# Recurrent mixer of a hybrid encoder: running values in PSUM banks, GELU as one table function, a fourth buffer of gate weights

## The chip, the cores and the metric

The kernel runs on one core of a Trainium2 chip. The metric is the device time of one execution in microseconds (us); the times below are the median, the lowest and the highest of three executions, and the time of one profiled execution. The engines are called as in the profile: PE (TensorE, matmul), DVE (VectorE), ACT (ScalarE), POOL (GpSimd), and SP, which issues the large transfers.

## What is computed

Input x has 256 tokens of 2048 channels, in fp32. There are two layers, each a token mixer followed by a SwiGLU feed-forward network, both with a residual. Mixer 0 is grouped-query attention; mixer 1, which the change touches, is a recurrent block:

```
xb, yb = split(h @ w_in)                       # 2 x 2048 channels
yb = gelu(yb, approximate=True)
xb = depthwise_conv_width_4(xb) + bias
for each direction d (forward, backward):
    r = sigmoid(xb @ w_a[d] + b_a[d])          # block diagonal, 8 blocks of 256 x 256
    i = sigmoid(xb @ w_i[d] + b_i[d])
    log_a = -8 * r * softplus(-lam[d]);  a = exp(log_a)
    u = sqrt(1 - a*a) * (i * xb)
    h_t = a_t * h_(t-1) + u_t                  # scan over the tokens
out = ((h_fwd + h_bwd) * yb) @ w_out
```

## The kernel before

Values lie with channels on the 128 partitions and the 256 tokens along the free axis, so one tile of 128 x 256 is a column of 128 channels. Matrix products run in two fp32r parts: a weight is split into hi and lo, an activation into a pair of halves, and three of the four products are summed. Weights stream in pieces of 512 KB (8 tiles of 128 x 128): a transfer on SP's queue (L92), a cast to hi on ACT (L93), a subtraction to lo on DVE (L94), with five buffers of each; PE follows. A product with 16 such tiles is 16 "steps".

In the recurrent mixer a column is projected by `project_sum`, 16 steps of three matmuls with 256 columns each (L166, L167, L168), into one half of a PSUM bank from the pool `acc` (4 banks). The mixer goes through 8 blocks of 256 channels, in 9 rounds: round b projects the two x columns of block b+1 (`conv_branch`) and then the two y columns of block b (`gelu_branch`), 64 steps in a full round, 240 matmuls with those of the gates.

- `conv_branch`: L535 brings the projection from PSUM to the tile cb, L537 (ACT) starts the convolution in xc, three operations of L539 (DVE) finish it, and `split` (L203, L204) makes xs, the input of the gates.
- `gelu_branch`: L547 brings y to SBUF, L549 (ACT) squares it, L550 (DVE) makes the argument of the sigmoid.
- `load_gates`: the weights of one gate (four per block: two of the decay, two of the input) by SP (L563), cast ghi on ACT (L564), glo on POOL (L565); three buffers of ghi and glo, two of the raw weights graw. The load of gate n+3 is written behind the matmuls of gate n.
- `Block.gates`: 12 matmuls into a PSUM bank of the pool `pm` (4 banks), then Sigmoid (sg); for the gates 2 and 3 a product with xc on POOL (L599), for the gates 0 and 1 a Tanh into th.
- `decay`: Exp and Square (L610) on ACT, L611 on DVE. `scan`: Sqrt on ACT, then L616 and the scan L619 or L621 on DVE, and h+h of both directions on POOL (L622).
- `gelu`: the table of Sigmoid is loaded (L576), Sigmoid of each y's argument, a product on POOL (L580) into gl. `finish`: a product on POOL (L627), and `split` makes the input of the output projection. In the last block the products of `gelu` and `finish` and h+h are on DVE (`self.eng`).

All functions that go through a table are issued by `table_act`, whose line is L298, and keep their written order; the load of a table stands on L298 too, except L576. PE's order is written by hand: `later(t, fn)` puts a piece of a block's work t steps after the start of its round (WHEN; WHEN_LAST in the last). Gates come at the steps 18, 25, 32 and 39, scans at 58 to 64, the end of the block at 66 to 74, so in the following round. The other engines take the order that a scheduler lays down at build time, and each works its queue in that order. The output projection (`output`) needs the last two columns only after 44 steps.

Of the kernel before, what the change touches and what calls it, by code (L numbers as in the profile page):

```python
# [14 lines left out]
AF = mybir.ActivationFunctionType  # L15
ALU = mybir.AluOpType
# [3 lines left out]
S = 256  # L20
D = 2048
KT = D // P
# [8 lines left out]
EPS = 1e-6  # L31
LRU_C = 8.0
GRID_W = 64
GELU_C = 0.7978845608028654

FRONT = 4
FIRST = 1
# [2 lines left out]
VALUE = 32  # L40
USUAL = (17, 22, 15, 7)
LATE = ((10, 23, 15, 13), (4, 15, 17, 9))
GATE_BUFS = 3
WHEN = (18, 25, 32, 39, 42, 46, 50, 54, 58, 60, 62, 64, 66, 70, 74)
WHEN_LAST = (5, 9, 13, 17, 19, 20, 21, 24, 24, 25, 26, 27, 33, 39, 39)
GELU_B = 0.044715

PK = {}
_o = 0
# [10 lines left out]
def trunk(ctx, tc, w, out):  # L60
    nc = tc.nc
    act, dve, pool, pe, sync = nc.scalar, nc.vector, nc.gpsimd, nc.tensor, nc.sync
# [87 lines left out]
    def new_acc():  # L150
        return ps_a.tile([P, 2 * S], F32, tag="acc", name=nm("acc"))
# [16 lines left out]
        pe.matmul(o, lo, x[:, :S], start=False, stop=stop)  # L168

    def project_sum(xs):  # L170
        acc = new_acc()[:, :S]
        for k0 in range(0, len(xs), HALF):
            for k, (hi, lo) in enumerate(half(), k0):
                three(acc, hi, lo, xs[k], k == 0, k == len(xs) - 1)
                step()
        return acc

    def output(xs, ready, norm, close):
        accs = [new_acc() for _ in range(FRONT)]
# [22 lines left out]
    def split(dst, src):  # L202
        dve.tensor_copy(dst[:, :S], src)  # L203
        dve.tensor_tensor(dst[:, S:], src, dst[:, :S].bitcast(F32), ALU.subtract)  # L204
# [3 lines left out]
    x_sb = [xq[k // 4][:, k % 4, :] for k in range(KT)]  # L208
# [13 lines left out]
    def col(name, i):  # L222
        o = PK[name] + i
        return pk[:, o : o + 1]
# [63 lines left out]
    def table_op(i):  # L288
        if prev[0] is not None:
            tc.add_manual_dep(  # L290
                i.ins, prev[0].ins.name,
                mybir.DependencyInfo(mybir.DependencyClass.NoSync, mybir.DependencyReason.DATA),
                reason="activation tables",
            )
        prev[0] = i

    def table_act(*a, **k):
        table_op(act.activation(*a, **k))  # L298
# [193 lines left out]
    def ffn(l, norm, nxt):  # L492
        def unit(i):
            g = evac(project(norm.xs), "fg")
            dve.tensor_tensor(g, g, norm.r, ALU.mult)
            table_act(g, g, AF.Silu)
            pool.tensor_tensor(g, g, norm.r, ALU.mult)  # L497
            u = evac(project(norm.xs), "fu")
            dve.tensor_tensor(u, u, g, ALU.mult)
            h = act_tile()  # L500
            split(h, u)
            return h

        bounds = np.cumsum([0] + PARTS)
        hid = [unit(i) for i in range(PARTS[0])]
        for p, n in enumerate(PARTS):
            last = p == len(PARTS) - 1
            cur = hid
            hid = [] if last else [unit(bounds[p + 1])]
            for j in range(KT):  # L510
                if last and j == KT - 1:
                    dve.tensor_tensor(x_sb[j], x_sb[j], project_sum(cur), ALU.add)
# [15 lines left out]
    rt = ctx.enter_context(ExitStack())  # L528
    scope.append(rt.enter_context(tc.tile_pool(name="rp", bufs=2)))
    def conv_branch(ct):  # L530
        acc = project_sum(nr.xs)
        b = tmp("cb", (P, S + 4))
        pool.memset(b[:, 0:2], 0.0)
        pool.memset(b[:, S + 2 : S + 4], 0.0)
        dve.tensor_tensor(b[:, 2 : S + 2], acc, nr.r, ALU.mult)  # L535
        xc = tmp("xc", bufs=4)
        act.activation(xc, b[:, 0:S], AF.Identity, bias=col("conv_b", ct), scale=col("conv_w", ct))  # L537
        for k in range(1, 4):
            dve.scalar_tensor_tensor(xc, b[:, k : k + S], col("conv_w", KT * k + ct), xc, ALU.mult, ALU.add)  # L539
        xs = tmp("xs", (P, 2 * S), F32R, bufs=4)  # L540
        split(xs, xc)
        return xc, xs

    def gelu_branch(ct):
        acc = project_sum(nr.xs)
        y = tmp("fg")
        dve.tensor_tensor(y, acc, nr.r, ALU.mult)  # L547
        t = tmp("fu")
        act.activation(t, y, AF.Square)  # L549
        dve.scalar_tensor_tensor(t, t, 1.0 / GELU_B, y, ALU.add, ALU.mult)  # L550
        return y, t


    gate_w = {}
# [13 lines left out]
    class Block:  # L568
        def __init__(self, b):
            self.b = b  # L570
            self.eng = pool if b < NBLK - 1 else dve
            self.xcs, self.ys, self.gls = [], [], []
            self.gate, self.th, self.hs = {}, {}, {}

        def gelu(self):
            table_op(act.preload_act_table_set("sigmoid_and_others"))  # L576
            for y, t in self.ys:
                table_act(t, t, AF.Sigmoid, scale=2.0 * GELU_C * GELU_B)
                gl = tmp("gl")
                self.eng.tensor_tensor(gl, y, t, ALU.mult)  # L580
                self.gls.append(gl)

        def gates(self, g):
            b = self.b
            hi, lo = gate_w.pop(4 * b + g)
            pst = ps_m.tile([P, 2 * S], F32, tag="pm", name=nm("pm"))
            for j in range(2):
                o = pst[:, j * S : (j + 1) * S]
                for k in range(2):
                    m = 2 * k + j  # L590
                    x = self.xcs[k][1]
                    three(o, hi[:, m, :], lo[:, m, :], x, k == 0, k == 1)
# [30 lines left out]
            self.hs.setdefault(j, h)  # L623

        def finish(self, j):
            h = self.hs[j]
            self.eng.tensor_tensor(h, h, self.gls[j], ALU.mult)  # L627
# [97 lines left out]
```

## Time and profile before

| | |
|---|---|
| median of 3 executions (lowest to highest) | 2129.33 us (2128.39 to 2139.98) |
| the profiled execution, its own time | 2129.33 us |
| its span in the trace (1.7 us lie outside) | 2127.6 us |
| busy: PE, DVE, ACT, POOL | 2085.5, 1502.9, 1050.4, 473.4 us |
| granted PE clock, mean over the span | 0.993 |
| PE in the stretch from 1063.3 to 1142.4 us | 79.10 of 79.10 us busy |
| PE in the stretch from 1142.4 to 1271.2 us | 120.34 of 128.80 us busy |
| PE in the stretch from 1271.2 to 1315.2 us | 36.63 of 44.00 us busy |

The page says that PE is busy for 98% of the whole span, which is a mean over stages. The recurrent mixer lies between 1063 and 1315 us: the last three rows are three stretches of it, and there PE is not always busy. A busy PE at a lower granted clock is busy for longer with the same work. Matmuls overlap in the trace, so the work of a stretch is best counted by the starts of its matmuls.

### The profile page before, as it was taken

The page shows a single profiled execution, that of the slowest core. Times are in us where ns is not written, and L with a number is a line of the kernel's source. Part 1 is how long each engine was busy: PE and PEld are TensorE (multiplying, and loading weights), DVE is VectorE, ACT ScalarE, POOL GpSimd, SP SyncE. Part 2 cuts the span into 40 slices and gives each one's busy share as a digit, 9 for nine tenths or more (in the row PEclk, how much of TensorE's full clock was granted, in tenths as well). Part 3 has the DMA queues.
Part 4 walks back from the last instruction along what each step waited for, and adds up shares of the span by engine and source line. Part 5 has one row for each costly group of instructions (what it writes and reads, how often), then busy time and mean ns, then how long its engine had stood idle before and what let it go on. Part 6 is the DMA issues. An engine that isn't in the chain of part 4 may idle for free.

```text
span 2127.6 us, 32676 instructions
## 1 busy us (share of the span) xinstructions
PE 2085.5 (98%) x12512; PEld 1848.4 (87%) x12512; DVE 1502.9 (71%) x2192; ACT 1050.4 (49%) x1598; POOL 473.4 (22%) x454
## 2 busy tenths in 40 slices
PE   7899999999999999999999998999999999999999
PEld 6788888888888888888999997888888888888888
DVE  8899876666566666668889898866666566666665
ACT  5465544443344434444587877454443444444442
POOL 5564431110011100113345553411110011001100
PEclk9999999999999999999999999999999999999999
DMA  6433655555555555555645454555555555665564
GB/s 239 146 122 118 203 187 189 185 185 186 187 188 188 173 186 195 188 183 177 196 160 169 161 166 157 185 188 190 190 194 189 189 189 187 183 203 190 188 189 138
DMA packets 112045, 384.27 MB, mean 181 GB/s; under 512 B 12560, under 2 KB 14736, under 8 KB 111888
## 3 DMA queue, kind: packets, MB, share of 16 engines
q1 hardware_dynamic: 111744, 382.17, 54.4%
q8 instruction: 98, 1.61, 0.3%
q14 instruction: 59, 0.48, 0.1%
q10 hardware_dynamic: 144, 0.02, 0.0%
HBM read 380.04 MB, written 2.10 MB: 180 GB/s over the span
## 4 chain that ended last, share of the span: by engine, by line
PE 86%; DVE 6%; issue 3%; ACT 2%; DMA 1%; POOL 1%; SPq 0%; ACTq 0%; DVEq 0%; POOLq 0%
PE acc L155 53%; PE acc L156 27%; DVE lo L94 2%; DMA graw<-in_w_gates_dram 1%; PE acc L168 1%; PE acc L167 1%; ACT sg L298 1%; PE acc L166 1%; PE pm L167 1%; POOL hb L351 1%; DVE xc L539 1%; PE pm L168 1%; DVE h L621 1%; ACT hi L93 1%; PE pm L166 1%
## 5 line engine op out<-in xcount | busy, mean ns | idle before, releaser
L94 DVE TENSOR_TENSOR lo<-raw,hi 128x1024 fp32r<-128x1024 f32 (+2 forms) x721 | 901.0, 1250 | 509.0 <-ACT hi L93 495.8
L93 ACT CAST hi<-raw 128x1024 fp32r<-128x1024 f32 (+2 forms) x721 | 740.8, 1029 | 928.2 <-PE acc L155 533.6
L155 PE MATMUL acc<-xg,hi 128*128 128x512 f32 x3200 | 1133.1, 398 | 5.7 <-ACT hi L93 5.7
L156 PE MATMUL acc<-xg,lo 128*128 128x256 f32 x3200 | 900.7, 281 | 5.4 <-DVE lo L94 5.4
L155 PEld LDWEIGHTS acc<-xg,hi 128*128 128x128 f32 x3200 | 603.4, 189 | 144.3 <-ACT hi L93 5.7
L155 PE MATMUL acc<-act,hi 128*128 128x512 f32 x1892 | 664.9, 396 | 4.6 <-DVE act L204 4.6
L156 PEld LDWEIGHTS acc<-xg,lo 128*128 128x128 f32 x3200 | 607.8, 190 | 7.1 <-DVE lo L94 7.0
L156 PE MATMUL acc<-act,lo 128*128 128x256 f32 x1892 | 530.9, 281 | 0.4 <-DVE lo L94 0.4
L155 PEld LDWEIGHTS acc<-act,hi 128*128 128x128 f32 x1892 | 355.8, 188 | 87.8 <-DVE act L204 5.5
L497 POOL TENSOR_TENSOR fg<-fg,nr 128x256 f32<-128x256 f32 x88 | 126.1, 1433 | 1189.9 <-ACT fg L298 1189.9
L156 PEld LDWEIGHTS acc<-act,lo 128*128 128x128 f32 x1892 | 358.4, 189 | 0.7 <-DVE lo L94 0.7
L168 PE MATMUL acc<-xg,lo 128*128 128x256 f32 x512 | 146.0, 285 | 3.0 <-DVE lo L94 3.0
L166 PE MATMUL acc<-xg,hi 128*128 128x256 f32 x512 | 146.4, 286 | 2.2 <-ACT hi L93 2.2
L167 PE MATMUL acc<-xg,hi 128*128 128x256 f32 x512 | 145.9, 285 | 0.0
L168 PEld LDWEIGHTS acc<-xg,lo 128*128 128x128 f32 x512 | 99.2, 194 | 3.8 <-DVE lo L94 3.8
L166 PEld LDWEIGHTS acc<-xg,hi 128*128 128x128 f32 x512 | 99.2, 194 | 3.1 <-ACT hi L93 3.1
L167 PEld LDWEIGHTS acc<-xg,hi 128*128 128x128 f32 x512 | 99.1, 194 | 0.0
L280 DVE TENSOR_TENSOR x<-x,acc 128x256 f32<-128x256 f32 x126 | 52.9, 420 | 57.8 <-PE acc L156 57.8
L254 POOL TENSOR_TENSOR ss<-ss,sq 128x256 f32<-128x256 f32 x60 | 78.1, 1302 | 4.9 <-ACT sq L250 0.7
L252 POOL TENSOR_TENSOR sq<-x 128x256 f32<-128x256 f32 x45 | 34.6, 769 | 114.6 <-DVE x L281 112.6
L244 DVE SCALAR_TENSOR_TENSOR xg<-x,pk,xg 128x256 fp32r<-128x256 f32 x64 | 56.2, 891 | 5.2 <-POOL xg L243 5.2
L351 POOL TENSOR_TENSOR hb<-hy,rope 32x256 f32<-32x256 f32 x60 | 46.1, 769 | 44.7 <-DVE hv L419 37.9
(164 smaller groups left out, 1486.6 us busy)
## 6 DMA issues: line engine op xcount, KB each, us to landing
raw<-in_w_gate_dram SPq DMA_DIRECT2D x176, 512.0 KB, 3.6
raw<-in_w_up_dram SPq DMA_DIRECT2D x176, 512.0 KB, 3.6
raw<-in_w_down_dram SPq DMA_DIRECT2D x128, 512.0 KB, 3.6
raw<-in_w_in_dram SPq DMA_DIRECT2D x64, 512.0 KB, 4.0
raw<-in_w_down_dram SPq DMA_DIRECT2D x64, 384.0 KB, 3.1
raw<-in_w_qv_dram SPq DMA_DIRECT2D x40, 512.0 KB, 3.7
raw<-in_w_o_dram SPq DMA_DIRECT2D x32, 512.0 KB, 3.6
raw<-in_w_out_dram SPq DMA_DIRECT2D x32, 512.0 KB, 3.7
```

The source lines that it names most:

```text
L93: act.copy(hi[:, sl, :], raw[:, sl, :])
L94: dve.tensor_tensor(lo[:, sl, :], raw[:, sl, :], hi[:, sl, :].bitcast(F32), ALU.subtract)
L155: pe.matmul(acc, hi, xs[k], start=(k == 0), stop=False)
L156: pe.matmul(acc[:, S:], lo, xs[k][:, :S], start=False, stop=(k == total - 1))
L166: pe.matmul(o, hi, x[:, :S], start=start, stop=False)
L167: pe.matmul(o, hi, x[:, S:], start=False, stop=False)
L168: pe.matmul(o, lo, x[:, :S], start=False, stop=stop)
L244: dve.scalar_tensor_tensor(t[:, S:], x_sb[k], g, t[:, :S].bitcast(F32), ALU.mult, ALU.subtract)
L254: pool.tensor_tensor(self.ss, self.ss, sq, ALU.add)
L280: dve.tensor_tensor(x_sb[j], x_sb[j], acc[:, :S], ALU.add)
L351: eng.tensor_tensor(b[32 * j : 32 * j + 32], y[32 * i : 32 * i + 32], s[32 * i : 32 * i + 32], ALU.mult)
L497: pool.tensor_tensor(g, g, norm.r, ALU.mult)
```

## The change

`project_sum` gives back, beside the half of the bank that holds the product, the other half, `run`. The running sum of the convolution lives there, and only its last step writes xc to SBUF; y lives there too (for the last two columns in SBUF, as the output projection takes all four banks then). L549 and L550 go. The GELU is one function from a table of its own, in place, in `run`. The Tanh's result th stays in the gate's PSUM bank, in place of the sigmoid's input, and with it L611's, the square root's and L616's results. The product of `finish` goes to DVE and its result into `run`, from where it is split; the products L580 and L627 on POOL go. The sigmoid's table is no longer loaded by L576: the loads stand where a function of another set follows, which makes four in a block (Sigmoid with Tanh, Exp, Sqrt, Gelu) where there were three. The gate weights have four buffers of ghi and glo.

```
-GATE_BUFS = 3
+GATE_BUFS = 4
...
     def project_sum(xs):
-        acc = new_acc()[:, :S]
+        bank = new_acc()
+        acc = bank[:, :S]
...
-        return acc
+        return acc, bank[:, S:]
...
-        acc = project_sum(nr.xs)
+        acc, run = project_sum(nr.xs)
...
-        act.activation(xc, b[:, 0:S], AF.Identity, bias=col("conv_b", ct), scale=col("conv_w", ct))
+        act.activation(run, b[:, 0:S], AF.Identity, bias=col("conv_b", ct), scale=col("conv_w", ct))
         for k in range(1, 4):
-            dve.scalar_tensor_tensor(xc, b[:, k : k + S], col("conv_w", KT * k + ct), xc, ALU.mult, ALU.add)
+            o = xc if k == 3 else run
+            dve.scalar_tensor_tensor(o, b[:, k : k + S], col("conv_w", KT * k + ct), run, ALU.mult, ALU.add)
...
     def gelu_branch(ct):
-        acc = project_sum(nr.xs)
-        y = tmp("fg")
+        acc, y = project_sum(nr.xs)
+        if ct >= KT - 2:
+            y = tmp("gl")
         dve.tensor_tensor(y, acc, nr.r, ALU.mult)
-        t = tmp("fu")
-        act.activation(t, y, AF.Square)
-        dve.scalar_tensor_tensor(t, t, 1.0 / GELU_B, y, ALU.add, ALU.mult)
-        return y, t
+        return y
...
         def gelu(self):
-            table_op(act.preload_act_table_set("sigmoid_and_others"))
-            for y, t in self.ys:
-                table_act(t, t, AF.Sigmoid, scale=2.0 * GELU_C * GELU_B)
-                gl = tmp("gl")
-                self.eng.tensor_tensor(gl, y, t, ALU.mult)
-                self.gls.append(gl)
+            for y in self.ys:
+                table_act(y, y, AF.Gelu_apprx_tanh)
...
-                    self.th[g, j] = tmp("th", bufs=4)
+                    self.th[g, j] = pst[:, j * S : (j + 1) * S]
...
         def finish(self, j):
-            h = self.hs[j]
-            self.eng.tensor_tensor(h, h, self.gls[j], ALU.mult)
-            split(g_t[2 * self.b + j], h)
+            y = self.ys[j]
+            dve.tensor_tensor(y, self.hs[j], y, ALU.mult)
+            split(g_t[2 * self.b + j], y)
```

PE's order stays, and so do the places of the casts and loads of weights in the queues of ACT and SP. Inside a block the scheduler lays the operations of ACT and DVE otherwise. ACT's queue from a block's square roots to the next convolution reads so before; hi and ghi are casts of weights, th the roots, fu the GELU's arguments:

```order
L93 CAST hi_11397<-raw_11396 128x1024
L298 ACT_TABLE_LOAD
L298 ACTIVATE th_10943<-th_10943 128x256
L298 ACTIVATE th_10997<-th_10997 128x256
L298 ACTIVATE th_10947<-th_10947 128x256
L298 ACTIVATE th_11001<-th_11001 128x256
L576 ACT_TABLE_LOAD
L298 ACTIVATE fu_11157<-fu_11157 128x256
L93 CAST hi_11492<-raw_11491 128x1024
L549 ACTIVATE fu_11249<-fg_11247 128x256
L93 CAST hi_11547<-raw_11546 128x1024
```

In the changed kernel the lines have lower numbers; pm_10911 and pm_10963 are the banks of the forward and the backward direction, each with the columns 0 and 1, and acc_11046 and acc_11141 hold the two y:

```order
L297 ACT_TABLE_LOAD
L297 ACTIVATE pm_10911<-pm_10911 128x256
L297 ACTIVATE pm_10963<-pm_10963 128x256
L91 CAST hi_11460<-raw_11459 128x1024
L297 ACTIVATE pm_10911<-pm_10911 128x256
L91 CAST hi_11515<-raw_11514 128x1024
L297 ACTIVATE pm_10963<-pm_10963 128x256
L297 ACT_TABLE_LOAD
L297 ACTIVATE acc_11046<-acc_11046 128x256
L297 ACTIVATE acc_11141<-acc_11141 128x256
L91 CAST hi_11555<-raw_11554 128x1024
L536 ACTIVATE acc_11229<-cb_11298,pk 128x256
```

The four roots, which stood together, now have a weight cast before the third and before the fourth; the third waits until DVE has scanned column 0 of its own bank, the fourth likewise. Both GELUs stand together behind their table.

DVE's queue at the same place before, from the first scan on (lo is a weight's subtraction, cb the next block's convolution):

```order
L619 SCALAR_TENSOR_TENSOR h_11213<-sg_1975_10941,th_10943 128x256
L621 SCALAR_TENSOR_TENSOR h_11223<-sg_1986_10995,th_10997 128x256
L619 SCALAR_TENSOR_TENSOR h_11234<-sg_1977_10945,th_10947 128x256
L621 SCALAR_TENSOR_TENSOR h_11244<-sg_1988_10999,th_11001 128x256
L94 TENSOR_TENSOR lo_11493<-raw_11491,hi_11492 128x1024
L550 SCALAR_TENSOR_TENSOR fu_11249<-fu_11249,fg_11247 128x256
L94 TENSOR_TENSOR lo_11548<-raw_11546,hi_11547 128x1024
L535 TENSOR_TENSOR cb_11326<-acc_11252,nr_10276 128x256
L203 CAST act_10217<-h_11213 128x256
```

And in the changed kernel, where L622 is the product of `finish`, with the result in the y's bank:

```order
L614 SCALAR_TENSOR_TENSOR h_11194<-sg_1968_10930,pm_10911 128x256
L92 TENSOR_TENSOR lo_11461<-raw_11459,hi_11460 128x1024
L616 SCALAR_TENSOR_TENSOR h_11204<-sg_1977_10982,pm_10963 128x256
L611 TENSOR_TENSOR pm_10911<-pm_10911,sg_1984_11031 128x256
L92 TENSOR_TENSOR lo_11516<-raw_11514,hi_11515 128x1024
L614 SCALAR_TENSOR_TENSOR h_11215<-sg_1969_10933,pm_10911 128x256
L611 TENSOR_TENSOR pm_10963<-pm_10963,sg_1997_11096 128x256
L622 TENSOR_TENSOR acc_11046<-h_11194,acc_11046 128x256
L534 TENSOR_TENSOR cb_11298<-acc_11229,nr_10276 128x256
L616 SCALAR_TENSOR_TENSOR h_11225<-sg_1978_10985,pm_10963 128x256
L202 CAST act_10217<-acc_11046 128x256
```

The scans, which stood in a row, are apart, with weights' subtractions between them; the product of column 0 stands ahead of the next convolution's start cb and of the last scan.

More of the change, by code (lines that the diff above doesn't have):

```diff
@@ L33 @@
 GRID_W = 64
-GELU_C = 0.7978845608028654
 FRONT = 4
@@ L42 @@
 LATE = ((10, 23, 15, 13), (4, 15, 17, 9))
-GATE_BUFS = 3
+GATE_BUFS = 4
 WHEN = (18, 25, 32, 39, 42, 46, 50, 54, 58, 60, 62, 64, 66, 70, 74)
 WHEN_LAST = (5, 9, 13, 17, 19, 20, 21, 24, 24, 25, 26, 27, 33, 39, 39)
-GELU_B = 0.044715
 PK = {}
@@ L511, in ffn @@
                 if last and j == KT - 1:
-                    dve.tensor_tensor(x_sb[j], x_sb[j], project_sum(cur), ALU.add)
+                    dve.tensor_tensor(x_sb[j], x_sb[j], project_sum(cur)[0], ALU.add)
                     if nxt is not None:
@@ L571, in __init__ @@
             self.eng = pool if b < NBLK - 1 else dve
-            self.xcs, self.ys, self.gls = [], [], []
+            self.xcs, self.ys = [], []
             self.gate, self.th, self.hs = {}, {}, {}
         def gelu(self):
-            table_op(act.preload_act_table_set("sigmoid_and_others"))
-            for y, t in self.ys:
-                table_act(t, t, AF.Sigmoid, scale=2.0 * GELU_C * GELU_B)
-                gl = tmp("gl")
-                self.eng.tensor_tensor(gl, y, t, ALU.mult)
-                self.gls.append(gl)
+            for y in self.ys:
+                table_act(y, y, AF.Gelu_apprx_tanh)
         def gates(self, g):
```

## The prediction

> **What bounds the kernel now.** I read the page first. PE is busy for 98% of the span, so a change off PE can only win where PE waits. The windows view of the recurrent mixer shows where that is (columns: us, then busy time and instructions of PE, of its weight loads, of DVE, ACT and POOL, the granted PE clock, DMA share, GB/s):
>
> ```profile
> PE 2085.5 (98%) x12512; PEld 1848.4 (87%) x12512; DVE 1502.9 (71%) x2192; ACT 1050.4 (49%) x1598; POOL 473.4 (22%) x454
> 1063.30:1142.40 79.10, 79.10 (x665) 79.10 (x664) 68.44 (x96) 62.99 (x113) 40.71 (x46) 1.00 0.52 170
> 1142.40:1271.20 128.80, 120.34 (x973) 118.09 (x973) 116.05 (x162) 102.76 (x182) 68.74 (x70) 0.99 0.50 164
> 1271.20:1315.20 44.00, 36.63 (x231) 33.37 (x231) 35.65 (x57) 34.17 (x62) 12.82 (x13) 0.90 0.40 133
> ```
>
> In the first stretch PE runs without a gap: 79.10/665 = 0.119 us a matmul, so a block of 240 matmuls takes 28.5 us. In the second it needs 128.80 us for 973, which at 0.119 are 115.7: 13.1 lost. In the tail 36.63 us are busy at a clock of 0.90, worth 33.0 at full clock: 11.0 lost of 44.0. **The most that this change can win is therefore about 24.1 us, 1.1% of the time.**
>
> The chain of waits over the stage returns at the same place in each block, the exponentials of the decay; the first and the last of seven:
>
> ```profile
> 1079.73 0.95 ACT sg L298 x3
> ...
> 1271.22 0.95 ACT sg L298 x3
> ```
>
> Six periods of 31.92 us: longer than PE's 28.5. So PE, which had run ahead of the others, is held from 1142 on by a loop on the other engines. PE's waits between 1043 and 1325 us name its outlets (total, times, longest):
>
> ```profile
> PE pm L168 <- POOL glo L565: 4.2, 4, 1.1
> PE acc L155 <- DVE act L204: 3.7, 1, 3.7
> PE acc L168 <- DVE lo L94: 3.0, 4, 0.8
> PE pm L166 <- ACT ghi L564: 2.3, 1, 2.3
> ```
>
> Gate weights come late, then weights, and at the end the last column of the mixer. One period of the chain shows what sets all of them (start, us, what):
>
> ```profile
> 1146.03 0.97 DVE lo L94
> ...
> 1149.73 0.34 DVE fu L550
> 1150.07 1.13 DVE lo L94
> ...
> 1155.22 1.17 DVE h L621
> ...
> 1157.50 0.88 DVE fu L550
> ...
> 1164.45 0.40 DVE xc L539
> ...
> 1164.85 0.34 DVE act L204
> ...
> 1165.99 2.09 issue
> ...
> 1168.56 4.89 DMA graw<-in_w_gates_dram
> ...
> 1173.55 0.62 ACT ghi L564
> ...
> 1174.93 1.28 ACT L298
> ...
> 1178.90 1.24 DVE lo L94
> ```
>
> DVE has no gap from 1146.03 until it frees a raw buffer at 1168.5 (22.5 us); SP, whose queue is in order, then gets to the gate's load (5.05 until ACT takes it); ACT casts it, and what stands behind in its queue follows (two sigmoids, a table load, the exponentials, a weight cast: 5.35), and DVE starts its next stretch at 1178.90. The sum is 32.87.
>
> **Part by part: DVE's stretch.** Some of DVE's time there is inflated. The "2.09 issue" is the end of a subtraction that took twice its time while POOL subtracted too; the timeline has the pair at 1134, and the groups show a quiet stage (480 to 640 us) against the recurrent one:
>
> ```profile
> 1134.11 1.31 POOL L565 TENSOR_TENSOR glo<-graw,ghi 128x512 fp32r<-128x512 f32 x1
> 1134.20 2.31 DVE L94 TENSOR_TENSOR lo<-raw,hi 128x1024 fp32r<-128x1024 f32 x1
> ```
> ```profile
> L94 DVE TENSOR_TENSOR lo<-raw,hi x57: 1224/1225/1226, 481.3 to 639.6; 128x1024 fp32r<-128x1024 f32 x57
> ```
> ```profile
> L94 DVE TENSOR_TENSOR lo<-raw,hi 128x1024 fp32r<-128x1024 f32 x40 | 55.6, 1391 | 15.8 <-ACT hi L93 15.8
> L616 DVE TENSOR_TENSOR th<-th,sg 128x256 f32<-128x256 f32 x20 | 7.5, 418 | 0.3
> L627 POOL TENSOR_TENSOR h<-h,gl 128x256 f32<-128x256 f32 x10 | 13.6, 1364 | 0.4
> L580 POOL TENSOR_TENSOR gl<-fg,fu 128x256 f32<-128x256 f32 x10 | 12.9, 1287 | 47.4 <-ACT fu L298 47.4
> ```
> ```profile
> L535 DVE TENSOR_TENSOR cb<-acc,nr x10: 409/411/416, 1128.3 to 1264.3; 128x256 f32<-128x256 f32 x10
> ```
> ```profile
> L539 DVE SCALAR_TENSOR_TENSOR xc<-cb,pk,xc x30: 472/839/1518, 1131.1 to 1267.8; 128x256 f32<-128x256 f32 x30
> ```
>
> An operation with two inputs in SBUF swings by a factor of three (L539), one with an input in PSUM stays within 409 to 416 ns whatever POOL does (L535). The change gives every DVE operation of this stretch but the subtractions of weights and the xs split an input in PSUM, and takes 2 of POOL's 13.6 us and 2 of its 12.9 us groups away: (13.6 + 12.9)/5 = 5.3 us a block.
>
> So I add the stretch up again at the undisturbed steps, from start to start: 7 weight subtractions at 1.13 (the row at 1150.07) are 7.9; 3 operations of L539 at 0.40 (at 1164.45) are 1.2; 18 small ones (4 of L611, 4 of L616, two evacuations, two products of `finish`, two splits and the xs split of two operations each) at 0.34 (at 1164.85) are 6.1; the four scans at 0.60, by a row of the tail:
>
> ```profile
> 1303.39 0.60 DVE h L619
> ```
>
> are 2.4. That makes 17.6, with the two products that come over from POOL (0.7) in it, and without L550, which took 0.34 + 0.88. What the subtractions still lose to POOL is today 7 x (1.391 - 1.225) = 1.2; a third of POOL's work goes, so I keep 0.8 (bounds 0 and 1.2). DVE's stretch becomes 18.4 instead of 22.5.
>
> *The price of PSUM.* About 22 of these operations read or write a PSUM bank that they did not. The nearest rows are L535, from PSUM, with 411 ns, against L616, from SBUF alone, with 418: I take zero. The widest gap between like operations of the two kinds is ACT's, 463 ns for a sigmoid from PSUM and 510 for a Tanh from SBUF:
>
> ```profile
> L298 ACT ACTIVATE sg<-pm,pk 128x256 f32<-128x256 f32 x40 | 17.5, 463 | 0.0
> L298 ACT ACTIVATE th<-sg,cs 128x256 f32<-128x256 f32 x20 | 10.2, 510 | 0.5
> L298 ACT ACT_TABLE_LOAD x10 | 12.8, 1283 | 0.2
> ```
>
> Taken in both directions, 22 x 0.047 = 1.0 us a block either way. [...]
>
> **ACT.** L549 goes (two a block) and a fourth table load of 1.28 us (the 1283 ns above) comes; the GELU takes the sigmoid's place. ACT was busy for some 25.4 us of a period (102.76/128.80 x 31.92) and stays under 26.8, so it fits a block. The new load, the sigmoid's, stands behind the cast of a gate's weights, right behind the convolution's start. ACT's timeline there, from the convolution that DVE's cb releases to the weight cast that DVE needs next:
>
> ```profile
> 1160.49 0.60 ACT L537 ACTIVATE xc<-cb,pk 128x256 f32<-128x256 f32 x1 [1.66 <-DVE cb L535]
> ...
> 1162.78 1.03 ACT L93 CAST hi<-raw 128x1024 fp32r<-128x1024 f32 x1
> ```
>
> is 3.3 us, with the load 4.6. DVE's own work between, one subtraction (1.13), three of L539 (1.2) and five small ones (1.7), comes to 4.0, so DVE waits 0.6 there (bounds 0 and 1.28). The third and fourth root each wait for a scan and the product of `finish` for the GELU; between them DVE has a weight subtraction (1.13) and ACT a cast, which cover the handshakes, and I price them at nothing; the rival below prices them uncovered.
>
> **The gate weights.** The fourth buffer means that each load, at its old place in the queues of SP and ACT, serves one gate later. That takes PE's waits on glo and ghi (4.2 + 2.3). But ACT's cast still stands in the same row and still waits for the same transfer, so the transfer and what follows it stay in the loop: 5.05 + 5.35. The extra first load lies before the feed-forward network, where DVE waits for ACT anyway; 0 to 1 us, I take 0.
>
> **New waits of PE.** The matmuls of gate 2 need the bank whose last reader is now the scan of forward, column 1:
>
> ```profile
> 1158.61 0.28 PE L166 MATMUL pm<-xs,ghi 128*128 128x256 f32 x1
> ```
>
> In the period shown all but the last scan have ended by 1155.3, so 3.3 us are left. A y column needs the bank that `finish` of the block before splits. From its first matmul to that split the loop runs over 7 steps and two gates, ACT's sigmoids and exponentials, and DVE's stretch up to the split (about 14 us): some 24 to 25 us, under the 28.5 of a block. Both are covered as long as DVE gains; uncovered, each would cost its lag once, not per block.
>
> **The sum.** 18.4 + 5.05 + 5.35 + 0.6 = 29.4 us a loop against 31.92 (this period had 32.87, so 29.4 is rather high): 6 x 2.5 = 15.1 us by the last exponentials. In the last block DVE sheds two of L550 and two of L580 from its chain:
>
> ```profile
> 1302.98 0.41 DVE fu L550
> ...
> 1305.17 0.40 DVE gl L580
> ```
>
> with 0.88 for the first L550, as at 1157.50, and 0.34 for the second product that is 2.0. Together 17.1 us of the 24.1 that PE loses: **2129.3 - 17.1 = 2112.2 us**. The profiled execution is the median of the runs, so nothing is to be converted. With the bounds (0 or 1.2 of contention, 1.0 of PSUM either way, 0 to 1.28 for the load) the loop lies between 27.0, where PE's 28.5 holds, and 31.5: 2105 to 2125.
>
> **The rivals.** *PE becomes the bound.* If the weight subtractions lose nothing more, or PSUM is a little cheaper, the loop falls under 28.5, PE runs as in the first stretch, and the tail shrinks as well: 2129.3 - 24.1 = 2105.2. For it speaks that the shown period was a long one; against it, that ACT gets up to 26.8 us busy of 28.5 and still has waits for DVE and for the transfer.
>
> *The loop stays.* The gate's transfer and the queue of ACT hold the block, and what POOL no longer reads, its subtractions and h+h take from DVE at other places (every weight subtraction can still go to 2318 ns). The loop is then 31, DVE's relief being lost but for one us: 6 x 0.9 + 2.0 = 7.4 less, some 2122, or with no relief at all 2127. For it speaks that ACT's idle time before the gate's cast is a wait for the transfer, which is not touched.
>
> *Slower: ACT's queue.* ACT works in order. Its third and fourth root now wait for scans with a weight subtraction ahead of each on DVE, and every weight cast behind them waits too, so that DVE lacks its next subtraction. If both handshakes lie bare, with subtractions at their longest (2.31 at 1134.20), the loop is 29.4 + 4.6 = 34.0: 6 x 2.1 - 2.0 = 10.6 slower, 2140. It decides from 2.5 us of bare wait a block. Against it speaks that ACT has idle time and five hi buffers. [...]
>
> **How the numbers follow.** The forecast has 0.42, PE as the bound 0.28, the loop that stays 0.21, slower 0.09. A measurement of this kernel can tell about 0.5%, 10.6 us, from no change. The first two cases lie under 2118.7, but for the upper end of the first, which the lower part of the third makes up: faster 0.69. Between 2118.7 and 2140.0 lie the third and half of the last: same 0.26; slower 0.05. The range goes from 2104, PE's bound with 1 us for its estimate, to 2126, the upper end of the forecast and all of the third case but its no relief at all.
>
> **What would show it.** Right: L539, the scans and the split at 0.40 to 0.70 us with no swing; periods of the exponentials at 29 to 29.8; PE's waits on glo and ghi gone; four loads of 1283 ns a block. Wrong: periods over 31 with DVE idle before weight subtractions and ACT idle before roots or casts (the third case or the last); PSUM operations of over 0.5 us; PE waiting for the bank of a y column or of gate 2 in every block.

## The result and the profile after

The changed kernel takes 2105.43 us (median of 4 executions, 2104.81 to 2106.43), the kernel before 2128.86 (2128.05 to 2139.98). The ratio is 0.9892, with a 95% interval of 0.9846 to 0.9937: 1.1% faster. The forecast was 2112.2 with a range of 2104 to 2126; the time came out where the rival "PE becomes the bound" had put it, 2105.2.

The windows view of three stretches of the recurrent mixer, after, from the first gate on (columns as before):

```profile
1063.00:1142.40 79.40, 79.40 (x667) 79.40 (x666) 62.14 (x103) 71.50 (x123) 30.09 (x40) 1.00 0.52 177
1142.40:1251.50 109.10, 109.10 (x916) 109.10 (x915) 94.07 (x155) 98.72 (x167) 42.46 (x51) 1.00 0.55 186
1251.50:1292.00 40.50, 39.57 (x287) 37.15 (x286) 30.38 (x54) 33.79 (x59) 5.89 (x8) 1.00 0.38 132
```

PE has no gap left in the loop, its clock is full, and its only wait between 1043 and 1325 us is one for the last column:

```profile
PE acc L153 <- DVE act L203: 0.9, 1, 0.9
```

To compare kernels, two numbers are taken from each trace. One is the stage, from the first matmul of a gate to the first of the second feed-forward network. PE's timeline has its two ends, of before:

```profile
1063.31 0.28 PE L166 MATMUL pm<-xs,ghi 128*128 128x256 f32 x1
...
1390.23 0.40 PE L155 MATMUL acc<-xg,hi 128*128 128x512 f32 x1
```

and of after:

```profile
1063.03 0.28 PE L164 MATMUL pm<-xs,ghi 128*128 128x256 f32 x1
...
1366.02 0.40 PE L153 MATMUL acc<-xg,hi 128*128 128x512 f32 x1
```

326.9 us became 303.0: the 23.9 us that the stage lost account for the whole gain (23.4 us between the medians). The other number is the length of six periods, from the first to the seventh start of a block's exponentials. The windows view over them, first of before, then of after (length; busy time of PE, its weight loads, DVE, ACT, POOL):

```profile
1079.32:1270.81 191.49, 183.03 (x1498) 180.78 (x1498) 172.00 (x241) 152.15 (x271) 100.85 (x105) 0.99 0.50 165
```
```profile
1079.00:1251.04 172.04, 172.04 (x1443) 172.04 (x1442) 146.69 (x240) 156.39 (x264) 64.49 (x81) 1.00 0.54 183
```

A period fell from 31.92 to 28.67 us, which is PE's own time for a block. In it DVE went from 28.7 busy us to 24.4 with the same number of instructions, POOL from 16.8 to 10.7, and ACT rose from 25.4 to 26.1. Stage and period are used below because whole executions of one kernel differ by some 13 us (2104.37 to 2106.52 and 2118.35 to 2119.89 for the changed kernel with three buffers), and between two traces most of that lies in the second feed-forward network and behind it, which the change does not touch: what follows the stage takes 738.6 us in the trace of the changed kernel and 749.9 in that of the changed kernel with three buffers. One trace was taken of each kernel. The changed kernel with four and with three buffers, both at PE's pace, agree to 0.01 us in the stage; how much the stage of an irregular loop varies from one execution to the next was not measured.

Where DVE's time went, by groups over five blocks (busy, mean ns, idle before). Two of before, 1112.1 to 1271.2 us:

```profile
L539 DVE SCALAR_TENSOR_TENSOR xc<-cb,pk,xc 128x256 f32<-128x256 f32 x30 | 26.9, 896 | 0.4
L619 DVE TENSOR_TENSOR_SCAN h<-sg,th 128x256 f32<-128x256 f32 x10 | 9.3, 925 | 0.0
```

After, 1108.5 to 1251.9 us, with some of ACT and POOL:

```profile
L92 DVE TENSOR_TENSOR lo<-raw,hi 128x1024 fp32r<-128x1024 f32 x40 | 53.8, 1345 | 10.4 <-ACT hi L91 8.8 <-DMA graw<-in_w_gates_dram 1.6
L297 ACT ACT_TABLE_LOAD x20 | 25.7, 1283 | 0.4
L563 ACT CAST ghi<-graw 128x512 fp32r<-128x512 f32 x20 | 12.2, 610 | 5.1 <-PE pm L165 5.1
L539 DVE SCALAR_TENSOR_TENSOR acc<-cb,pk,acc 128x256 f32<-128x256 f32 x20 | 9.6, 482 | 0.2
L611 DVE TENSOR_TENSOR pm<-pm,sg 128x256 f32<-128x256 f32 x20 | 7.9, 415 | 0.3
L617 POOL TENSOR_TENSOR h<-h,h 128x256 f32<-128x256 f32 x10 | 7.4, 740 | 66.1 <-DVE h L616 66.1
L614 DVE TENSOR_TENSOR_SCAN h<-sg,pm 128x256 f32<-128x256 f32 x10 | 6.8, 675 | 0.0
L549 DVE TENSOR_TENSOR acc<-acc,nr 128x256 f32<-128x256 f32 x11 | 4.7, 428 | 11.4 <-PE acc L166 11.4
```

The convolution's steps fell from a mean of 896 ns to 482, and the scans from 925 to 675, with no more rows of 1.17 us as in the period shown before. DVE now waits for PE (11.4 us over five blocks, ahead of L549): PE paces DVE, no longer the other way round.

### The profile page after: what moved, and what is told of

It reads as the page before. It is cut to its first block, busy times and chain, and to the rows that moved or that the text cites. A ratio compares the mean times of both kernels' runs of the same rounds, so it can differ in the third digit from the quotient of the medians.

```text
span 2104.6 us, 32732 instructions
## 1 busy us (share of the span) xinstructions
PE 2077.5 (99%) x12512; PEld 1838.3 (87%) x12512; DVE 1470.5 (70%) x2188; ACT 1054.8 (50%) x1589; POOL 433.0 (21%) x426
## 4 chain that ended last, share of the span: by engine, by line
PE 94%; DVE 2%; issue 2%; POOL 1%; ACT 1%; DMA 0%; SPq 0%; DVEq 0%; POOLq 0%; ACTq 0%
PE acc L153 54%; PE acc L154 27%; PE acc L164 3%; PE acc L165 3%; PE acc L166 3%; PE pm L165 1%; PE pm L166 1%; PE pm L164 1%; DVE lo L92 1%; POOL hb L350 1%; PE pm L437 0%; ACT L297 0%; DMA x<-in_x_dram 0%; ACT sg L297 0%; POOL ss L253 0%
## 5 line engine op out<-in xcount | busy, mean ns | idle before, releaser
L496 POOL TENSOR_TENSOR fg<-fg,nr 128x256 f32<-128x256 f32 x88 | 126.0, 1432 | 1190.0 <-ACT fg L297 1190.0
L165 PE MATMUL acc<-xg,hi 128*128 128x256 f32 x512 | 144.6, 282 | 0.0
L165 PEld LDWEIGHTS acc<-xg,hi 128*128 128x128 f32 x512 | 97.9, 191 | 0.0
L564 POOL TENSOR_TENSOR glo<-graw,ghi 128x512 fp32r<-128x512 f32 x32 | 52.0, 1625 | 31.9 <-ACT ghi L563 31.8
```

The source lines that it names most:

```text
L165: pe.matmul(o, hi, x[:, S:], start=False, stop=False)
L564: pool.tensor_tensor(lo, raw, hi[:].bitcast(F32), ALU.subtract)
```

## The experiments

Two theories stood against each other at first. **A**: what held the loop was DVE's stretch, lengthened by POOL's reading of SBUF, and the change shortens it by placement and by taking work off POOL. **B**: PE's waits for the gate weights were the loss, and the fourth buffer was the gain. Further rivals come with the runs.

**The fourth buffer taken back.** The changed kernel with `GATE_BUFS = 3`.

```
-GATE_BUFS = 4
+GATE_BUFS = 3
```

> The changed kernel with three buffers of gate weights as before. Theory A: DVE's stretch of some 18 us frees the weight buffers early enough, periods of 28.7 stay and the time is 2105 to 2108; at most PE waits a little for glo. Rival B: the wait for glo and ghi comes back with 1 us or more a block, periods of 29.5 to 31, and 2112 to 2122.

The ratio to the kernel before on that chip was 0.9847 (0.9819 to 0.9876), the stage 303.0 us, the six periods:

```profile
1081.22:1253.22 172.00, 172.00 (x1442) 172.00 (x1442) 146.18 (x240) 156.39 (x265) 64.50 (x81) 1.00 0.57 184
```

28.67 us a period and the same stage to 0.1 us: the fourth buffer is worth nothing here. B falls.

**th in PSUM, with and without the fourth buffer, on the kernel before.** th in PSUM also makes the room that a fourth buffer needs in SBUF: its four tiles of 128x256 hold as many values as one more ghi and glo of 128x512.

```
-                    self.th[g, j] = tmp("th", bufs=4)
+                    self.th[g, j] = pst[:, j * S : (j + 1) * S]
```

> The kernel before, with two parts of the change alone: th lies in the gate's PSUM bank, which makes room in SBUF for the fourth buffer of gate weights. Theory A (what counted is DVE's stretch, which POOL's reading had lengthened and which L550 and the SBUF operands of convolution and finish belong to): the scans and L611, L616 no longer swing, which is 1 us a block, PE's waits on glo and ghi go, but the periods of the exponentials stay at 30.5 to 31.5 us, and the time falls by 3 to 9 us, to 2120 to 2126. Rival B (the fourth buffer took PE's waits away and that was the gain): periods of 28.7, and 2105 to 2110.

> The kernel before with th in the gate's PSUM bank alone and three buffers of gate weights, to divide the kernel with both (periods of 30.3 to 31.7, 10.5 us less for the stage from the first gate to the second feed-forward network). Theory A: placement is what helped, since L611, L616 and the scans no longer swing; the stage is 6 to 11 us shorter. Rival B: the fourth buffer was what helped there; the stage is 0 to 4 us shorter.

With both: ratio 0.9953 (0.9929 to 0.9976), periods of 30.3 to 31.7 with a mean of 30.94, stage 316.4, 10.5 less than before. With th alone: 0.9944 (0.9919 to 0.9970), mean 31.12, stage 317.4, 9.5 less. So it is th's move that helped, by 9.5 us, and the fourth buffer by some 1.0 there. Three groups of the kernel with th alone show a part of how:

```profile
L611 DVE SCALAR_TENSOR_TENSOR pm<-sq,pm 128x256 f32<-128x256 f32 x23 | 8.6, 422 | 0.0
L616 DVE TENSOR_TENSOR pm<-pm,sg 128x256 f32<-128x256 f32 x20 | 7.7, 423 | 0.2
L619 DVE TENSOR_TENSOR_SCAN h<-sg,pm 128x256 f32<-128x256 f32 x10 | 6.7, 675 | 0.0
```

L616 and L611 were not inflated before (418) and cost the same from PSUM; the scans lost their swing. But a change of place also changes the order that the scheduler lays down: in this kernel the scans stand in two pairs with a weight subtraction between them, where before all four stood together, and the products of POOL fell from 1364 and 1287 ns to 767 and 744. The 9.5 us are those of th's place together with this order; no run divides the two. The new wait that comes with it shows once, in both kernels, with 5.9 us: PE's gate 2 waits for the scan that was the last reader of its bank.

```profile
PE pm L166 <- DVE h L619: 5.9, 1, 5.9
```

**The convolution alone**, its running sum in the other half of the bank, on the kernel before.

```
-        act.activation(xc, b[:, 0:S], AF.Identity, bias=col("conv_b", ct), scale=col("conv_w", ct))
+        act.activation(run, b[:, 0:S], AF.Identity, bias=col("conv_b", ct), scale=col("conv_w", ct))
...
+            o = xc if k == 3 else run
-            dve.scalar_tensor_tensor(xc, b[:, k : k + S], col("conv_w", KT * k + ct), xc, ALU.mult, ALU.add)
+            dve.scalar_tensor_tensor(o, b[:, k : k + S], col("conv_w", KT * k + ct), run, ALU.mult, ALU.add)
```

> The kernel before with the running sum of the convolution in the other half of the bank alone. Theory A: L539 falls from a mean of 0.90 us to under 0.50, 2.5 us a block of DVE's time, of which what lies in DVE's stretch counts (1 to 2 us): periods of 30 to 31, the stage 6 to 12 us shorter. If POOL's reading only moves to the next operations with two inputs in SBUF: periods of 31.3 to 32, the stage 0 to 3 us shorter.

Ratio 0.9987 (0.9958 to 1.0015), periods 31.44 in the mean, stage 323.8, 3.1 less. The expectation of theory A was missed; the other one, that POOL's reading only moves to other operations, was met but for 0.1 us of the stage. The queues of DVE and ACT keep their order here, so this is the one run in which place alone is changed. In two groups of that trace the operations themselves did what was said:

```profile
L94 DVE TENSOR_TENSOR lo<-raw,hi 128x1024 fp32r<-128x1024 f32 x41 | 56.9, 1387 | 26.5 <-ACT hi L93 26.5
L541 DVE SCALAR_TENSOR_TENSOR acc<-cb,pk,acc 128x256 f32<-128x256 f32 x20 | 9.6, 479 | 0.2
```

The first steps (L541 there, L539 before) fell from a mean of 896 to 479 ns and DVE's busy time a period from 28.7 to 26.9, but its wait for ACT's casts rose from 15.8 to 26.5 us over the window: three of the six steps lie behind the point where the gate's load is released (1169.88 against 1168.56 in the period shown before), and were beside the transfer anyway. The subtractions kept their time, 1387 ns, and the casts of h rose from 387 to 733 ns, which takes back a part of what the steps gave.

**The GELU alone**, on the kernel before: one function, y in SBUF, the product of `finish` still on POOL.

```
-        t = tmp("fu")
-        act.activation(t, y, AF.Square)
-        dve.scalar_tensor_tensor(t, t, 1.0 / GELU_B, y, ALU.add, ALU.mult)
-        return y, t
+        return y
...
-            table_op(act.preload_act_table_set("sigmoid_and_others"))
-            for y, t in self.ys:
-                table_act(t, t, AF.Sigmoid, scale=2.0 * GELU_C * GELU_B)
-                gl = tmp("gl")
-                self.eng.tensor_tensor(gl, y, t, ALU.mult)
-                self.gls.append(gl)
+            for y in self.ys:
+                table_act(y, y, AF.Gelu_apprx_tanh)
+                self.gls.append(y)
```

> The kernel before, with the GELU as one table function alone: no Square, no L550, no product L580 on POOL, four table loads, y in SBUF, and the product of finish still on POOL. Theory A: DVE loses two L550 (1.2 us) and what two of POOL's products took from it (about 1 us), so periods of 29.5 to 30.5 and 2113 to 2121. Rival C (the fourth table load on ACT eats it): periods of 31 to 32, 2125 to 2131. Rival D (POOL's products were all of it): 28.7 and 2106 to 2110.

Ratio 0.9947 (0.9927 to 0.9966), mean period 30.88, stage 313.1, 13.8 less. The stage fits A; the periods, 30.1 to 31.7, lie above what it expected, and 2.6 us come from the last block, whose period fell from 24.1 to 21.5. The fourth table load did not eat the gain (C). POOL's products were not all of it (D): the run further down that moves both pairs of them gives 14.9 of the 23.9 us.

**All but the placement**: the changed kernel with the convolution's sum, y and th in SBUF and three buffers. It is read beside the changed kernel with three buffers.

```
+        run = xc
         act.activation(run, b[:, 0:S], AF.Identity, bias=col("conv_b", ct), scale=col("conv_w", ct))
...
-        if ct >= KT - 2:
-            y = tmp("gl")
+        y = tmp("gl")
...
-                    self.th[g, j] = pst[:, j * S : (j + 1) * S]
+                    self.th[g, j] = tmp("th", bufs=4)
```

> The changed kernel, but with the running sum of the convolution, y and th in SBUF, and three buffers of gate weights, since the room does not suffice for four; GELU and the product of finish on DVE as changed. To be read beside the changed kernel with three buffers: the difference is the placement alone. Theory A: POOL's reading inflates L539, scans and split again (L539 with maxima of over 1 us), DVE's stretch is longer by 2 to 3 us, periods of 29.5 to 30.5 and 2112 to 2120. Rival E (fewer operations on DVE and POOL were enough): periods of 28.7 and 2105 to 2109, placement worth nothing.

Ratio 0.9879 (0.9850 to 0.9909), mean period 29.41, stage 307.2. Three groups and the six periods of that trace:

```profile
L540 DVE SCALAR_TENSOR_TENSOR xc<-cb,pk,xc 128x256 f32<-128x256 f32 x30 | 23.4, 779 | 0.5
L202 DVE CAST act<-gl 128x256 fp32r<-128x256 f32 x10 | 8.3, 832 | 0.0
L614 DVE TENSOR_TENSOR_SCAN h<-sg,th 128x256 f32<-128x256 f32 x10 | 6.8, 683 | 0.0
```
```profile
1080.63:1257.10 176.47, 176.47 (x1479) 176.47 (x1479) 161.64 (x239) 155.54 (x265) 66.79 (x80) 1.00 0.56 179
```

DVE is busy for 26.9 us of a period, 2.6 more than with the values in PSUM, as A had it; but the scans stay at 683, with POOL idle for 51.9 us over five blocks ahead of its h+h, up to the end of a scan (L616). The placement, with the order of the queues that comes with it, is worth 4.2 us of the stage where the other parts are in (307.2 to 303.0), and the other parts 19.7 by themselves. Rival E falls by the stage and the periods; the ratios of whole executions alone, 0.9879 and 0.9847, have intervals that overlap. PE is not held within these periods: it starts 1479 matmuls in them, 39 more than six blocks have, and runs ahead of the loop, as it did before up to 1142 us; it pays at the end, when it needs the mixer's last columns.

**POOL's products on DVE, nothing else**, on the kernel before.

```
-                self.eng.tensor_tensor(gl, y, t, ALU.mult)
+                dve.tensor_tensor(gl, y, t, ALU.mult)
...
-            self.eng.tensor_tensor(h, h, self.gls[j], ALU.mult)
+            dve.tensor_tensor(h, h, self.gls[j], ALU.mult)
```

> The kernel before with the two pairs of products, of gelu and of finish, on DVE in place of POOL in all blocks, nothing else. DVE gets 4 operations of 0.34 to 0.42 us more a block, POOL 5.3 us less. Without contention the loop would get longer by 1.4 us: periods of 33 and over, the stage 6 to 9 us longer. Theory A: what POOL's products took from DVE comes back and outweighs it, and the hop over POOL goes: periods of 30 to 31.9, the stage 0 to 12 us shorter.

Ratio 0.9934 (0.9903 to 0.9965), mean period 29.44, stage 312.0, 14.9 less. The six periods, and the weight subtractions (1112 to 1257 us):

```profile
1080.93:1257.58 176.65, 176.65 (x1481) 176.65 (x1481) 168.43 (x264) 151.30 (x271) 79.90 (x80) 1.00 0.55 179
```
```profile
L94 DVE TENSOR_TENSOR lo<-raw,hi 128x1024 fp32r<-128x1024 f32 x40 | 48.7, 1216 | 4.7 <-ACT hi L93 4.7
```

DVE has 23 instructions more than before (264 against 241) and is busy for less: 168.43 us against 172.00. The subtractions are back at 1216 ns from 1391. So they take less time where POOL does less (79.90 us busy against 100.85 over six periods), without any placement in PSUM. That is not the whole of the gain, though: DVE's busy time fell by 0.6 us a period and the period by 2.5. The rest are waits, DVE's for ACT's casts (15.8 us over five blocks before, 4.7 here) and ACT's for the gate's transfer (below); this run does not divide what DVE's shorter operations gave to that from what a freer POOL gave. The steps of L539, whose two tiles lie in SBUF here as before, took 864 ns (896 before); with one of the two in PSUM they took 479 in the kernel with the convolution alone and 482 in the changed kernel.

Side by side, the parts that take work off POOL, alone on the kernel before, are worth 13.8 us (the GELU, which also takes two operations off DVE) and 14.9 us (the products). Placement is worth 3.1 us (the convolution, order unchanged), 9.5 us (th, order changed) and 4.2 us at the end. The larger part of the gain, 19.7 of 23.9 us, comes without placement, from the GELU and POOL's products together.

**The loop with a quicker PE.** Three kernels, with one execution each, leave out the middle of the three matmuls in the recurrent projections (the high part of the weight with the low part of the activation), 64 of a block's 240.

```
-                three(acc, hi, lo, xs[k], k == 0, k == len(xs) - 1)
+                pe.matmul(acc, hi, xs[k][:, :S], start=(k == 0), stop=False)
+                pe.matmul(acc, lo, xs[k][:, :S], start=False, stop=(k == len(xs) - 1))
```

> The changed kernel with the same matmuls left out. My sum on record gave the loop 29.4 us, which PE's 28.67 a block can't show. If the sum holds, the periods are 29 to 30 (against 28.67 measured, so that is out already but for its lower end). Theory A': the gate's transfer has left the loop, since the weight buffers come free by 4 us earlier and ACT's cast finds it landed; then 18.0 of DVE and ACT's 5.35 and waits remain, and ACT with 26.1 us busy sets 26.1 to 27.5. Rival F: ACT's waits for the scans and GELU make it 27.5 to 28.6, so that PE's bound was all but met by a second one.

> The kernel before, with the middle one of the three matmuls of every step left out in the projections of the recurrent mixer (the product of the weight's high part with the activation's low part), so that PE needs 176 instead of 240 matmuls a block, 21 us, and the loop of the other engines stands bare. If the periods of the exponentials, 31.9 us before, are set by DVE, the gate transfer and ACT without PE, they stay at 31 to 32.5. If PE is in the loop, they fall with PE's own time, to 27 to 30.

> The changed kernel with the running sum of the convolution, y and th in SBUF and three buffers of gate weights (periods of 29.1 to 29.6 with all matmuls), and with the same matmuls left out. If its loop is DVE's, lengthened by POOL, the periods stay at 29 to 29.6 and DVE is busy for over 95% of them; if PE is in it, they fall to 26 to 28.

The changed kernel settles at 27.40 us a period (28.2, 27.8, then four of 27.4). My sum of 29.4 is out. But neither A' nor F named what holds it. PE's waits over six periods show one place:

```profile
PE pm L164 <- DVE h L615: 27.7, 6, 4.6
```

4.6 us in each block, for the bank of gate 2, which the scan of forward, column 1, still reads: th's place in PSUM has closed a loop through PE (scan, the bank of gate 2, gate 3, ACT's cast of gate weights, exponentials, root, the scan again). That PE's wait reaches ACT can be seen at that cast: ACT waits 0.9 to 1.8 us ahead of it, and in each of the six blocks it starts 0.08 to 0.09 us after the end of PE's last matmul of L165. ACT is busy for 25.7 of 27.6. The kernel before, with the same matmuls left out, is irregular (27.0 to 37.2, mean 30.7), so it does not decide whether PE is in its loop. The kernel with the values in SBUF swings too (26.3 to 30.9, mean 28.1), between its two expectations; DVE is busy there for 98% of the six periods (165.98 of 168.81) against 84% (138.64 of 165.62) in the changed kernel:

```profile
1062.94:1231.75 168.81, 141.91 (x1098) 138.67 (x1097) 165.98 (x242) 157.27 (x267) 84.38 (x80) 0.94 0.58 191
```
```profile
1066.41:1232.03 165.62, 137.91 (x1059) 136.69 (x1058) 138.64 (x241) 154.32 (x264) 74.47 (x82) 0.92 0.58 190
```

So with a quicker PE the placement takes 4.6 us a block off DVE, but the time does not follow: the mean period is 27.6 against 28.1, the stage 298.5 us with the values in PSUM and 297.9 with them in SBUF, and the whole execution 2085.9 against 2082.4. The wait for the bank of gate 2, which th in SBUF does not have, may be what eats DVE's gain; no run shows that by itself.

**More table loads.** The changed kernel with one more load a block behind the GELU (the first added line), and with two.

```
             for y in self.ys:
                 table_act(y, y, AF.Gelu_apprx_tanh)
+            table_op(act.preload_act_table_set("natural_log_exp_and_others"))
+            table_op(act.preload_act_table_set("sqrt_and_others"))
```

> The changed kernel with two more table loads a block behind the GELU (2.57 us more on ACT, nothing else). ACT's busy time becomes 26.07 + 2.57 = 28.6 of PE's 28.67 a block, and ACT had 2.6 us idle there, of which about 1 us are waits for the scans. Theory A' and F agree that ACT is the next bound: periods of 29 to 30.5, and 2107 to 2117. If ACT had real slack beyond the idle time seen (waits that only took up room), the periods stay at 28.67. [...]

> The changed kernel with one more table load a block behind the GELU (1.28 us). With two the periods were 29.53, 0.86 over PE's 28.67, so 1.71 of the 2.57 us fitted in: one fits, the periods stay at 28.67, and the stage from the first gate to the second feed-forward network is 303 to 305 us long (302.98 without). If instead each load adds from the first on, the periods are 29.1.

Two loads: ratio 0.9931 (0.9903 to 0.9959), periods of 29.52 to 29.53, stage 309.8. One: 0.9905 (0.9875 to 0.9936), a mean period of 28.92, stage 307.8. The first expectation was met. The second was missed: 28.92 lies between its two values, and the stage is 2.8 us above its upper end, so one load does not fit whole. Of the first 1.28 us a period shows 0.25, of the second 0.61 more, and of the stage's 4.8 us for one load 1.5 lie in the six periods and the rest outside them. Taken off again, the loads leave ACT's loop at 27.0 (29.53 - 2.57) to 27.6 (28.92 - 1.28): by this estimate ACT is a next bound, 1.0 to 1.7 us away.

## Why the prediction was right, and where it was not

The time lay in the range because the range reached down to PE's bound, a rival that had 0.28. The sum itself gave 2112.2, by a loop of 29.4 us that would still hold PE; it came out shorter, and PE's 28.67 held. So the right range is not owed to the forecast's own mechanism.

- **The ceiling** of 24.1 us: the stage gave 23.9, and PE waits 0.9.
- **DVE's stretch**, 18.4 us: from the first weight subtraction of the stretch, at 1167.72 in DVE's timeline after, to the end of the seventh, 1184.51 + 1.23, it is 18.0. The sum had the split of xs (0.7) in it, which now follows that end, so like stands against like with 17.7 and 18.0.

```profile
1167.72 1.22 DVE L92 TENSOR_TENSOR lo<-raw,hi 128x1024 fp32r<-128x1024 f32 x1 [1.62 <-ACT hi L91]
...
1184.51 1.23 DVE L92 TENSOR_TENSOR lo<-raw,hi 128x1024 fp32r<-128x1024 f32 x1
```

  What the subtractions still lose is 7 x (1.345 - 1.225) = 0.84, where I kept 0.8.
- **PSUM at no price**: products and scans, yes (L611 415 ns against 418, the scans 675). L549, which now writes PSUM too, rose from 414 to 428. The casts of h, no: 400 ns from PSUM against 280 for one from SBUF while POOL was idle (the last section).
- **ACT fits**: 26.1 us of 28.67. The roots wait 1.0 us a block for the scans (2.9 + 2.0 us over five), and no period shows it. Twenty loads took 1283 ns each with 0.4 us idle before them in all.
- **The step that failed** is the sum of what follows DVE's stretch, "the transfer and what follows it stay in the loop: 5.05 + 5.35", with 0.6 of waiting added. ACT's timeline at the place of the cast that had waited 2.79 us for the gate's transfer, before:

```profile
1173.55 0.62 ACT L564 CAST ghi<-graw 128x512 fp32r<-128x512 f32 x1 [2.79 <-DMA graw<-in_w_gates_dram]
```

  and after:

```profile
1189.19 0.83 ACT L297 ACTIVATE sg<-pm,pk 128x256 f32<-128x256 f32 x2
1191.03 0.62 ACT L563 CAST ghi<-graw 128x512 fp32r<-128x512 f32 x1 [1.02 <-PE pm L165]
```

  The order of the queues is the old one, as I had said, but not the times. SP's queue, before (1168.56) and after (1186.93):

```profile
1168.18 0.33 SPq L92 DMA_DIRECT2D raw<-in_w_in_dram  x1
1168.56 1.21 SPq L563 DMA_DIRECT2D graw<-in_w_gates_dram  x1
```
```profile
1185.77 0.33 SPq L90 DMA_DIRECT2D raw<-in_w_in_dram  x1
1186.93 0.33 SPq L562 DMA_DIRECT2D graw<-in_w_gates_dram  x1
```

  Before, the load went out right behind the weight transfer in front of it, which had waited for DVE, 0.87 us ahead of the cast before last at 1169.43. After, it goes out 1.75 us ahead of its counterpart at 1188.68, and what it waited for was POOL's reading of the buffer, which ended at 1186.90:

```profile
1185.47 1.43 POOL L564 TENSOR_TENSOR glo<-graw,ghi 128x512 fp32r<-128x512 f32 x1 [0.97 <-ACT ghi L563]
```

  It took 3.3 us to land, at 1190.2, where the one before took 4.89. ACT had come to it at 1190.0 and could take it at 1191.03, when PE had done with a buffer of ghi. So the transfer is not gone: from the end of DVE's stretch it lands after 4.5 us, 0.2 us after ACT comes, and PE's wait hides it. With ACT's 5.35 up to DVE's next stretch at 1196.38, the loop without PE would be 18.0 + 4.5 + 5.35 = 27.9 us, an estimate, near the 27.4 of the kernel with fewer matmuls, whose loop has PE in it. My 29.4 was 1.5 too long, in three terms. The stretch was 0.4 shorter. The transfer's 5.05 came from the period with the longest one: the same load took 3.5 to 3.7 us in the other four between 1130 and 1270, and ACT waited 1.4 to 1.6 us for it instead of 2.79. And the 0.6 did not come: DVE has no wait ahead of its subtraction at 1184.51, and one of 0.46 us ahead of the next lies beside the transfer. The prediction had seen that its period was a long one and left it so: 32.87 - 31.92 = 0.95 off 29.4 is 28.4, under PE's 28.67.

  ACT's wait for this transfer, between 1080 and 1252 us, was 9.6 us before, 7.6 to 9.3 in the kernels with th, the convolution or the GELU alone, 0.6 with POOL's products on DVE, 0.5 with all but the placement and none after. It goes where both pairs of products have left POOL, wherever the values lie; no run divides this further.
- **The first rival** had the time, but not its reason: the subtractions still lose 0.84 us, and PSUM is no cheaper. It won because the sum was too long in the three terms above.
- **The fourth buffer at nothing**: right, though not for the reason that the transfer keeps its full length in the loop. PE's waits on glo and ghi went because ACT and POOL came in time; with three buffers they went too.
- **The new waits of PE**: covered, as said. How near the bank of gate 2 lies was not said: a PE faster by 1.3 us a block (28.67 - 27.40, an estimate) would meet it, and then in every block (4.6 us in each above), where the prediction had its lag once.
- **The slower rival**: its handshakes cost ACT 1.0 us of waiting a block. It needed 2.5 us of bare wait to lose to the kernel before; two added loads put 2.57 us on ACT, and the period of 29.53 is still 2.4 under 31.92. That a longer queue of ACT becomes the bound is shown by the kernels with more loads; that bare handshakes would, no run shows.

## What to carry to other kernels

Where POOL works beside DVE, look for the DVE operations whose time swings: moving four products a block from POOL to DVE made DVE's busy time shorter here (168.4 us against 172.0 over six blocks), and an accumulator kept in an idle half of a PSUM bank made its own steps short (479 ns from 896), though alone it brought 3.1 us. When a link of a loop gets shorter, ask of each following link what releases its start and who waits for its end before adding it at full length; put end to end, the links made the loop 1.5 us too long here, and the floor was the engine that had been waiting, PE. A period to add up is best taken near the mean: the one used here was 0.95 us longer. Parts that won 3 to 15 us each alone did not add up once that floor was met.

## What the runs showed of the hardware

An operation of POOL took less time as well: h+h, whose two instances took 1.13 and 1.64 us in the period shown before (1379 ns in the mean), took 740 ns in the mean after, with the same operands. A cast from PSUM took longer than one from SBUF beside an idle POOL: those of h in `split` took 387 ns in the mean from SBUF, with 280 at 1164.17 in the period shown before, where POOL was idle, and 400 in the mean from PSUM, with 409 at 1183.45 after, where POOL was idle too. A cast from SBUF to SBUF, with one input only, was long beside POOL: that of xs rose from a mean of 537 to 974 ns, and the one at 1185.65, beside POOL's subtraction of gate weights at 1185.47, took 1.40 us.

```profile
L202 DVE CAST xs<-xc 128x256 fp32r<-128x256 f32 x10 | 9.7, 974 | 0.2
L202 DVE CAST act<-acc 128x256 fp32r<-128x256 f32 x10 | 4.0, 400 | 0.0
```
